# Attention with bias: another order for the first casts, transposes and loads

## The chip, the cores and the metric

The kernel runs on one core of one Trainium2 chip. The metric is the device time of the whole program in microseconds (us), which is some 2 us more than the span of its instructions in the profile. All runs told here are of the state called fast; the one kernel that was run a single time has the state unknown.

## The reference

Four batches of eight heads, 1024 queries and keys, head width 64, with one bias matrix for all heads:

```python
scores = scale * np.matmul(q, k.transpose(0, 1, 3, 2))
scores = scores + bias
attn = np.exp(scores - scores_max) / (np.sum(np.exp(scores - scores_max), ...) + 1e-8)
return np.matmul(attn, v)
```

## The kernel before

The heads are taken in pairs, and for each head, half of the queries and chunk of 128 keys there is one *bank* of scores, 128 keys by 512 queries: 512 banks in all. ScalarE takes the exp of three banks at a time, VectorE multiplies it by the exp of the bias (so the bias is never added), TensorE multiplies by v.

```python
def s_exp(g):
    n = len(slots[g])
    nc.scalar.activation(e_at(slots[g][0], n), open_ps.pop(("S", g))[:, :n, :], ACTF.Exp, scale=scale)
```

Score group S0 has one bank, S1 two, S2, S3 and so on three each. Two score tiles of three banks alternate, so group n+2 can be filled when the exp of group n has ended. Before S0 the first pair must be cast to bfloat16, transposed on TensorE and copied from PSUM, where TensorE's results lie. Four small loads on the queues of SyncE and ScalarE bring it in float32; the second halves of k and q come by GpSimd, straight to bfloat16:

```python
nc.sync.dma_start(out=k0f[:, :, :2]...)      # k chunks 0-1
nc.scalar.dma_start(out=q0f[0]...)           # first half of the queries, head 0: "first q half"
nc.sync.dma_start(out=q0f[1]...)             # the same, head 1: "second q half"
nc.sync.dma_start(out=k0f[:, :, 2:]...)      # k chunks 2-3
# ... (cut)
nc.gpsimd.dma_start(out=kr0[:, :, QC:, :]...)    # k chunks 4-7
nc.gpsimd.dma_start(out=qr0[:, :, QC:, :]...)
nc.gpsimd.dma_start(out=btraw[:, :QC, :], in_=bf_[:, :QC, :])   # half of the bias, 1 MB
# ... (cut)
for i in range(6):                            # warm-up of TensorE
    nc.tensor.matmul(wm[:, i % 3, :], zeros[:, :P], zeros[:], start=True, stop=True)
# ... (cut)
k_first(0, nc.scalar.copy, nc.scalar.copy, "xb")    # cast, transpose, copy of chunks 0-1
c_a = q_first(0, "xa")                              # cast on VectorE, transpose
c_b = q_first(1, "xb")
c_a(); c_b()                                        # copies of q on VectorE
s_fill(0); s_exp(0)
k_first(2, nc.vector.tensor_copy, nc.vector.tensor_copy, "xa")
s_fill(1); s_exp(1)
nc.vector.memset(vall[:, :, :, D:D1], 1.0)
# four memsets of mask, on VectorE
```

Everything after that is put in order by a small plan in the program, which simulates the three engines with fixed costs and emits instructions in that order (constants `COLD`, `T0` and others).

The softmax here doesn't subtract the row's maximum and nothing guards it: scores larger than these inputs give would overflow.

## Time and profile before

| | before |
|---|---|
| time, median of 6 runs | 251.59 us (251.08 to 251.86) |
| span in the profile | 249.4 us |
| busy: ScalarE, TensorE, VectorE | 239.0, 229.8, 220.4 us |
| exp of S0, S1, S2, S3 starts at | 5.77, 7.06, 7.98, 10.60 |
| last exp ends at | 244.40 |

The start times are those of the ACTIVATE records, counted from the start of the span. From S3 on ScalarE runs without a wait, so the table's fourth row decides. TensorE's clock is part of the trace too: its record of full clock begins at 4.65 us in this profile. Before that the matmuls show half: in the warm-up they have a pitch (start to start) of 0.43 us. The column PEclk of the views doesn't show it, as it says 1.00 where there is no record.

### The profile page before, as it was taken

How to read it: one execution, taken by the hardware profiler on the slowest of the kernel's cores; microseconds unless marked ns; L12 is line 12 of the kernel's file. 1: busy time of each engine (PE TensorE's matmuls, PEld its weight loads, DVE VectorE, ACT ScalarE, POOL GpSimd, SP SyncE). 2: the span in 40 equal slices, each digit the busy share in tenths (PEclk: the TensorE clock that was granted, in tenths of full speed). 3: DMA queues.
4: the chain of work that ended last, by engine and by line, in shares of the span. 5: the costliest groups of instructions: out<-in, count | busy, mean ns of one | idle time of the engine just before them, and what ended most of it. 6: DMA issues, size and time to landing. Idle time of an engine off the chain costs nothing.

```text
span 249.4 us, 7171 instructions
## 1 busy us (share of the span) xinstructions
PE 229.8 (92%) x3152; PEld 141.3 (57%) x3152; DVE 220.4 (88%) x380; ACT 239.0 (96%) x180; POOL 52.6 (21%) x72
## 2 busy tenths in 40 slices
PE   6668999999999999999999999999999999999893
PEld 2245656556666556666556556566565555665552
DVE  4519799999999999999999999999999999988884
ACT  4799999999999999999999999999999999999991
POOL 6653304260130221302213055016000000000000
PEclk9999999999999999999999999999999999999998
DMA  7999989699194493921925769629901102020112
GB/s 147 194 205 186 192 90 141 55 158 160 45 147 67 86 105 95 99 88 24 178 49 95 85 83 184 75 87 114 110 33 43 45 0 88 3 84 3 62 46 64
DMA packets 48175, 23.79 MB, mean 95 GB/s; under 512 B 34448, under 2 KB 44048, under 8 KB 47888
## 3 DMA queue, kind: packets, MB, share of 16 engines
q0 software_dynamic: 42272, 14.42, 52.9%
q1 hardware_dynamic: 5584, 8.72, 9.8%
q8 instruction: 24, 0.39, 0.6%
q10 hardware_dynamic: 288, 0.20, 0.3%
q14 instruction: 7, 0.06, 0.1%
HBM read 29.36 MB, written 8.39 MB: 151 GB/s over the span
## 4 chain that ended last, share of the span: by engine, by line
ACT 77%; PE 13%; DVE 5%; issue 2%; DMA 1%; DVEq 0%; ACTq 0%
ACT E L136 74%; PE ps L129 10%; ACT eb L149 3%; PE po L186 2%; DVE E L161 2%; PE px L89 1%; DMA k0f<-in_k_dram 1%; DVE mask L271 1%; DVE E L155 1%; DVE qT L98 1%; DVE kT L102 0%; DVE oall L206 0%; PE px L247 0%; DVE rs L196 0%; DVE qT L255 0%
## 5 line engine op out<-in xcount | busy, mean ns | idle before, releaser
L136 ACT ACTIVATE E<-ps 128x1536 bf16<-128x1536 f32 (+2 forms) x172 | 230.1, 1707 | 2.7 <-PE ps L129 2.7
L129 PE MATMUL ps<-qT,kT 128*128 128x512 bf16 x512 | 138.2, 377 | 10.4 <-ACT E L136 4.7
L186 PEld LDWEIGHTS <-E 128*128 128x128 bf16 x2048 | 83.2, 98 | 38.3 <-DVE E L158 1.6
L158 DVE TENSOR_TENSOR E<-E,eb 128x2048 bf16<-128x2048 bf16 x81 | 97.6, 1216 | 1.1 <-ACT E L136 0.7
L186 PE MATMUL po<-vall,E 128*128 128x65 bf16 x2048 | 92.8, 194 | 1.4 <-DVE E L158 0.5
L129 PEld LDWEIGHTS <-kT 128*128 128x128 bf16 x512 | 45.2, 96 | 43.8 <-issue 7.2
L161 DVE TENSOR_TENSOR E<-E,eb 128x1024 bf16<-128x1024 bf16 x86 | 57.1, 683 | 6.7 <-ACT eb L149 5.6
L75 POOL DMA_DIRECT2D kr<-in_k_dram x15 | 10.5, 701 | 94.6 <-PE px L89 93.4
L81 POOL DMA_DIRECT2D vall<-in_v_dram x32 | 28.1, 883 | 7.4 <-DMA btraw<-in_bias_dram 3.7
L206 DVE TENSOR_TENSOR oall<-po,rs 128x256 f32<-128x256 f32 x63 | 26.7, 424 | 2.2
L98 DVE TENSOR_TENSOR qT<-px,mask 128x1024 bf16<-128x1024 bf16 x31 | 21.3, 686 | 3.7 <-PE px L89 3.1
L102 DVE COPY kT<-px 128x512 bf16<-128x512 bf16 x31 | 13.0, 421 | 2.5 <-PE px L89 2.1
L196 DVE RECIPROCAL rs<-po 128x4 f32<-128x4 f32 x64 | 11.3, 177 | 4.1 <-PE po L186 3.6
L76 POOL DMA_DIRECT2D qr<-in_q_dram x15 | 10.8, 717 | 18.8 <-PE px L89 16.8
L89 PE MATMUL px<-ident,kr 128*64 128x128 bf16 x248 | 12.8, 225 | 0.3 <-DVE oall L206 0.3
L89 PE MATMUL px<-ident,qr 128*64 128x128 bf16 x248 | 12.8, 225 | 0.0
L89 PEld LDWEIGHTS <-qr 128*64 128x64 bf16 x248 | 7.9, 109 | 7.9 <-issue 6.8
L89 PEld LDWEIGHTS <-kr 128*64 128x64 bf16 x248 | 7.9, 109 | 7.1 <-issue 5.5
L149 ACT ACTIVATE eb<-pb 128x2048 bf16<-128x2048 bf16 x4 | 7.5, 1877 | 0.0
L144 PE MATMUL pb<-ident,btraw 128*128 128x128 bf16 x64 | 4.6, 225 | 1.8 <-ACT E L136 0.9
L144 PEld LDWEIGHTS <-btraw 128*128 128x128 bf16 x64 | 4.6, 147 | 2.3 <-issue 2.0
L155 DVE TENSOR_TENSOR E<-E,eb 128x1024 bf16<-128x1024 bf16 (+1 forms) x6 | 4.6, 774 | 0.6 <-ACT E L136 0.6
(36 smaller groups left out, 20.3 us busy)
## 6 DMA issues: line engine op xcount, KB each, us to landing
out_dram<-oall SPq DMA_DIRECT2D x30, 256.0 KB, 2.0
vall<-in_v_dram POOLq DMA_DIRECT2D x32, 128.0 KB, 6.3
kr<-in_k_dram POOLq DMA_DIRECT2D x15, 256.0 KB, 4.0
qr<-in_q_dram POOLq DMA_DIRECT2D x15, 256.0 KB, 5.5
btraw<-in_bias_dram POOLq DMA_DIRECT2D x2, 1024.0 KB, 9.8
out_dram<-oall SPq DMA_DIRECT2D x3, 128.0 KB, 1.7
k0f<-in_k_dram SPq DMA_DIRECT2D x2, 128.0 KB, 3.4
q0f<-in_q_dram ACTq DMA_DIRECT2D x1, 128.0 KB, 2.6
```

The source lines that it names most:

```text
L81: nc.gpsimd.dma_start(out=vall[:, 2 * pr + t, :, :D], in_=vf[pr, :, t])
L89: nc.tensor.transpose(px[t * D:(t + 1) * D, c, :], src[:, t, half * QC + c, :], ident[:])
L98: nc.vector.tensor_tensor(dst[:, :, half * HQ:(half + 1) * HQ], px.rearrange("p c q -> p (c q)").unsqueeze(1).to_broadcast([P, 2, HQ]), ma ...
L102: nc.vector.tensor_copy(dst[:, half * QC:(half + 1) * QC, :], px[:])
L129: nc.tensor.matmul(ps[:, j, :], kT[:, kc, :], qT[:, h, qh * HQ:(qh + 1) * HQ], start=True, stop=b not in late_bias)
L136: nc.scalar.activation(e_at(slots[g][0], n), open_ps.pop(("S", g))[:, :n, :], ACTF.Exp, scale=scale)
L149: nc.scalar.activation(eb[:, qh, k0:k0 + 4, :], open_ps.pop(("B", qh, k0))[:, :4, :], ACTF.Exp)
L158: nc.vector.tensor_tensor(e, e, eb[:, qh, kc:kc + 2, :].unsqueeze(2).to_broadcast([P, 2, 2, HQ]), op=ALU.mult)
L161: nc.vector.tensor_tensor(e, e, eb[:, qh, kc:kc + 1, :].to_broadcast([P, n, HQ]), op=ALU.mult)
L186: nc.tensor.matmul(acc[:, i, :], e[:, 0, i * P:(i + 1) * P], vall[:, 2 * pr + h, kc, :], start=(kc == 0 and i == 0), stop=(kc == NCH - 1), ...
L196: nc.vector.reciprocal(rs[:], acc[:, :, D:D1])
L206: nc.vector.tensor_tensor(oall[:, c0:c0 + QC, :], acc[:, :, :D], rs[:].to_broadcast([P, QC, D]), op=ALU.mult)
```

## The change

The intent is an earlier S0 and an unbroken stream behind it: only k chunk 0 is needed for S0, so it is handled alone; the second q half is cast on ScalarE and transposed into a score tile, so that it no longer waits for a PSUM tile; the memsets of the mask go behind the copy that S3 waits for; k chunks 2-3 move to ScalarE's queue. One warm-up matmul goes, and the plan gets new constants.

```diff
-        nc.sync.dma_start(out=k0f[:, :, 2:]..., in_=kf[0][:, :, 2 * D:QC * D])
+        nc.scalar.dma_start(out=k0f[:, :, 2:]..., in_=kf[0][:, :, 2 * D:QC * D])
@@
-        for i in range(6):
+        for i in range(5):
@@ (helpers cut)
-        k_first(0, nc.scalar.copy, nc.scalar.copy, "xb")
-        c_a = q_first(0, "xa")
-        c_b = q_first(1, "xb")
-        c_a()
-        c_b()
+        nc.scalar.copy(kr0[:, :, 0, :], k0f[:, :, 0, :])
+        nc.vector.tensor_copy(qr0[:, 0, :QC, :], q0f[0][:])
+        nc.vector.tensor_copy(kr0[:, :, 1, :], k0f[:, :, 1, :])
+        nc.scalar.copy(qr0[:, 1, :QC, :], q0f[1][:])
+        pq0 = q_trans(0, ps_x.tile(..., tag="xa", name="px"))
+        pk0 = k_trans(0, 1, "xb")
+        q_out(0, pq0)
+        nc.scalar.copy(kT0[:, :1, :], pk0[:])
+        pq1 = q_trans(1, ps_s.tile(..., tag="s", name="pq")...)
+        nc.vector.tensor_copy(kr0[:, :, 2:QC, :], k0f[:, :, 2:, :])
         s_fill(0)
+        q_out(1, pq1)
         s_exp(0)
-        k_first(2, nc.vector.tensor_copy, nc.vector.tensor_copy, "xa")
+        pk1 = k_trans(1, 1, "xb")
+        nc.vector.tensor_copy(kT0[:, 1:2, :], pk1[:])
+        pk2 = k_trans(2, 2, "xa")
         s_fill(1)
+        nc.vector.tensor_copy(kT0[:, 2:QC, :], pk2[:])
         s_exp(1)
@@
-        for t in range(2):
-            for u in range(2):
-                nc.vector.memset(mask[t * D:(t + 1) * D, u, :], 1.0 if t == u else 0.0)
@@
-        COLD = 9500
+        COLD = 6000
-        T0 = 6200.0
-        t_act, t_pe, t_dve = T0 + 700, T0, T0 + 500
+        T0 = 6000.0
+        t_act, t_pe, t_dve = T0 + 1400, T0 + 600, T0 + 1300
@@ (in the plan, behind the copy of the second half of k)
+                    if (pr, which, half) == (0, 1, 1):
+                        for x in range(2):
+                            for y in range(2):
+                                nc.vector.memset(mask[x * D:(x + 1) * D, y, :], 1.0 if x == y else 0.0)
```

More of the change, by code (lines that the diff above doesn't have):

```diff
@@ L218 @@
         nc.sync.dma_start(out=q0f[1].rearrange("p c d -> p (c d)"), in_=qf[0][:, 1, :QC * D])
-        nc.sync.dma_start(out=k0f[:, :, 2:].rearrange("p t c d -> p t (c d)"), in_=kf[0][:, :, 2 * D:QC * D])
+        nc.scalar.dma_start(out=k0f[:, :, 2:].rearrange("p t c d -> p t (c d)"), in_=kf[0][:, :, 2 * D:QC * D])
         nc.vector.memset(warm[:], 0.0)
@@ L237, with k_trans @@
         wm = ps_s.tile([P, 3, HQ], F32, tag="s", name="wm")
-        for i in range(6):
+        for i in range(5):
             nc.tensor.matmul(wm[:, i % 3, :], zeros[:, :P], zeros[:], start=True, stop=True)
-        def k_first(c0, eng_cast, eng_copy, tag):
-            cs = slice(c0, c0 + 2)
-            eng_cast(kr0[:, :, cs, :], k0f[:, :, cs, :])
-            px = ps_x.tile([P, 2, P], BF, tag=tag, name="px")
-            for c in range(2):
+        def k_trans(c0, n, tag):
+            px = ps_x.tile([P, n, P], BF, tag=tag, name="px")
+            for c in range(n):
@@ L246, in k_first, with q_trans @@
                 for t in range(2):
                     nc.tensor.transpose(px[t * D:(t + 1) * D, c, :], kr0[:, t, c0 + c, :], ident[:])
-            eng_copy(kT0[:, cs, :], px[:])
-        def q_first(t, tag):
-            nc.vector.tensor_copy(qr0[:, t, :QC, :], q0f[t][:])
-            px = ps_x.tile([P, QC, P], BF, tag=tag, name="px")
+            return px
+        def q_trans(t, px):
             for c in range(QC):
                 nc.tensor.transpose(px[t * D:(t + 1) * D, c, :], qr0[:, t, c, :], ident[:])
-            return lambda: nc.vector.tensor_copy(qT0[t * D:(t + 1) * D, t, :HQ],
-                                                 px[t * D:(t + 1) * D, :, :].rearrange("p c q -> p (c q)"))
@@ L258, with q_out @@
-        k_first(0, nc.scalar.copy, nc.scalar.copy, "xb")
-        c_a = q_first(0, "xa")
-        c_b = q_first(1, "xb")
-        c_a()
-        c_b()
+            return px
+        def q_out(t, px):
+            nc.vector.tensor_copy(qT0[t * D:(t + 1) * D, t, :HQ],
+                                  px[t * D:(t + 1) * D, :, :].rearrange("p c q -> p (c q)"))
+        nc.scalar.copy(kr0[:, :, 0, :], k0f[:, :, 0, :])
+        nc.vector.tensor_copy(qr0[:, 0, :QC, :], q0f[0][:])
+        nc.vector.tensor_copy(kr0[:, :, 1, :], k0f[:, :, 1, :])
@@ L263 @@
+        nc.scalar.copy(qr0[:, 1, :QC, :], q0f[1][:])
+        pq0 = q_trans(0, ps_x.tile([P, QC, P], BF, tag="xa", name="px"))
+        pk0 = k_trans(0, 1, "xb")
+        q_out(0, pq0)
+        nc.scalar.copy(kT0[:, :1, :], pk0[:])
+        pq1 = q_trans(1, ps_s.tile([P, 3, 2 * HQ], BF, tag="s", name="pq").rearrange(
+            "p b (c q) -> p (b c) q", q=P)[:, :QC, :])
+        nc.vector.tensor_copy(kr0[:, :, 2:QC, :], k0f[:, :, 2:, :])
         s_fill(0)
+        q_out(1, pq1)
         s_exp(0)
-        k_first(2, nc.vector.tensor_copy, nc.vector.tensor_copy, "xa")
+        pk1 = k_trans(1, 1, "xb")
@@ L285 @@
         NO = len(order)
-        T0 = 6200.0
-        t_act, t_pe, t_dve = T0 + 700, T0, T0 + 500
+        T0 = 6000.0
+        t_act, t_pe, t_dve = T0 + 1400, T0 + 600, T0 + 1300
         filled = []
         act_end = []
-        x_free = {"xa": T0 + 500, "xb": T0}
+        x_free = {"xa": T0 + 400, "xb": T0}
         x_unit = {}
@@ L301 @@
         eb_at = {}
-        exp_at = {0: T0, 1: T0 + 700, 2: T0 + 700}
+        exp_at = {0: T0, 1: T0 + 1400, 2: T0 + 1400}
         mul_at = {}
```

## The prediction

> **What bounds the kernel now.** I read the page from the top: the busy table, the 40 slices, the chain of waits. Then the waits of ScalarE, then the timeline of the first 16 us.
>
> ```profile
> PE 229.8 (92%) x3152; PEld 141.3 (57%) x3152; DVE 220.4 (88%) x380; ACT 239.0 (96%) x180; POOL 52.6 (21%) x72
> ACT  4799999999999999999999999999999999999991
> ACT 77%; PE 13%; DVE 5%; issue 2%; DMA 1%; DVEq 0%; ACTq 0%
> ```
>
> ScalarE (ACT) is the fullest engine, and its row of slices says where it is not full: the first two slices (one is 249.4/40 = 6.2 us) and the last. The view of who waited for whom, for ScalarE alone, has all its waits:
>
> ```profile
> ACT E L136 <- PE ps L129: 2.7, 3, 1.2
> ACT L222 <- PEq L534: 1.2, 1, 1.2
> ACT kr L243 <- DMA k0f<-in_k_dram: 0.9, 1, 0.9
> ACT kT L248 <- PE px L247: 0.5, 1, 0.5
> ```
>
> All of them lie in the start. The exp waited three times for scores, 2.7 us in all. The timeline shows where (start, length, engine, line, what; in brackets the idle time before it and what ended that):
>
> ```profile
> 4.53 0.37 ACT L248 COPY kT<-px 128x256 bf16<-128x256 bf16 x1 [0.52 <-PE px L247]
> 4.89 0.92 DVE L255 COPY qT<-px 64x512 bf16<-64x512 bf16 x2 [0.50 <-PE px L254]
> 5.77 0.60 ACT L136 ACTIVATE E<-ps 128x512 bf16<-128x512 f32 x1 [0.86 <-PE ps L129]
> 5.84 0.29 DVE L243 CAST kr<-k0f 128x256 bf16<-128x256 f32 x1
> 7.06 2.37 ACT L136 ACTIVATE E<-ps 128x1024 bf16<-128x1024 f32 x2 [0.70 <-PE ps L129]
> 8.00 1.67 DVE L271 MEMSET mask<- 64x512 bf16 x4
> 9.69 0.42 DVE L102 COPY kT<-px 128x512 bf16<-128x512 bf16 x1
> 10.60 4.13 ACT L136 ACTIVATE E<-ps 128x1536 bf16<-128x1536 f32 x3 [1.17 <-PE ps L129]
> ```
>
> Call the score groups S0 (one bank), S1 (two), S2, S3 and so on (three each). S0 starts at 5.77, S1 at 7.06, S2 follows it at once and ends at 9.43. S3 waits to 10.60, because its third score matmul needs the second half of the transposed k, and that copy (L102) stood behind four mask memsets on VectorE. The chain says the same:
>
> ```profile
> 8.00 0.48 DVE mask L271
> 9.18 0.48 DVE mask L271
> 9.69 0.44 DVE kT L102
> 10.18 0.40 PE ps L129
> 10.60 5.48 ACT E L136 x4
> ```
>
> After that ScalarE never waits. The busy time in stretches gives 40.00 of 40.00 us from 11 to 51 and full stretches up to 228. From 10.60 to its last end at 244.4 are 233.8 us. The work in it is 168 groups of three banks (169 in the form list, less S2) at a pitch of 1.342 us (5.48 for the four after 10.60 is 4 x 1.342 and an overlap), 225.5; the last group of two banks, 1.1; four bias exps of 1.77, 7.1; sum 233.7. So next to nothing is lost in 234 us. **Everything after S3's start is a fixed stream. What the change is worth is how much earlier S3 starts, less any hole that the stream gets later.** All the idle before 10.60 is some 5 us, 2% of 251.6, so faster by over 2% is nearly out of reach from the outset.
>
> **What the Trainium skill says.** (1) "ScalarE: Activation LUTs", What ACT_TABLE_LOAD costs: an ACTIVATE with immediate scale takes 186 ns + 0.833 ns an element, back-to-back ones overlap by about 93 ns, a table load takes about 1283 ns. At 1536 elements that is 1466 ns, 1373 with overlap. The trace has 1.45 and the 1.342 pitch, and 1.28 for the table load: it agrees within 3%. So the stream has no fat that this change could touch. (2) "TensorE: Matmul & The Clock Gate", What's actually happening: the array runs at half clock until about 3.4 us of activity. The trace agrees: warm-up matmuls from 1.23 at a pitch of 0.43, and from about 4.6 on the pitch of score matmuls is 0.216. One of six warm-up matmuls less ends them at 3.54, not 3.97; the first transposes then follow at about 3.73, a hole of 0.2 us, so I expect the full clock at about the same time. (3) "DMA: Bandwidth & Descriptors", Queues, rings and completion order: each DMA engine takes turns among the queues that have work, packet by packet. In the trace the k transfer that SyncE issued third (1.75) took 3.9 us to land, at 5.65, where the other three took 2.6 to 2.8: it shared the engines with the loads of GpSimd from 1.44 on. On ScalarE's queue it is issued at about 1.2, ahead of them. I expect it at 4.2 to 4.5.
>
> **The change part by part** (times in us from the span's start; what has no duration of its own in the trace is scaled, and marked est.).
> - First cast of ScalarE: 128 elements and not 256. 256 took 0.40 and the one-element warm exp 0.20, so 0.30 (est.): 3.61 to 3.91. Then the q1 cast on ScalarE, 0.40 from its landing. That was 3.91; beside the moved k transfer I take 4.05: done 4.45.
> - TensorE: q0 transposes first, 3.73 to 4.16 (four at half clock took 0.43 at L247); k chunk 0 done by 4.40; q1 transposes 4.50 to 4.90. They write a score tile, so they no longer wait for the k copy to free its bank (before: copy ended at 4.91, transposes began at 4.96).
> - Copies: q0 on VectorE 4.20 to 4.63 (0.43 in the chain), k chunk 0 on ScalarE 4.48 to 4.75 (est. 0.27). S0's matmul 4.95 to 5.33 (0.38), so the exp of S0 starts at **5.37, 0.4 earlier**.
> - VectorE: cast of k chunks 2-3 at 4.65 to 4.94 if landed, q1 copy 4.98 to 5.40, k chunk 1 copy 5.48 to 5.73, chunks 2-3 copy 5.75 to 6.04 (each 0.29 or less in the trace). S1's second matmul starts at 5.87, ends 6.25: exp of S1 at **6.28, 0.8 earlier**. S1 takes 0.92 to the start of S2 (7.06 to 7.98): S2 7.20, S2's end and S3's earliest start 8.55.
> - The four memsets (1.67) now stand behind the copy L102. The copy waits only for its transposes. TensorE has S2's fill to about 6.95, the eight k transposes (issued 1.44, 4.4 to landing, so 5.8) to 7.33, and, new in the instruction order, the eight q transposes (2.27 + 4.2, so 6.5) before S3's fill, to 7.75. L102 runs at 7.37 to 7.80. S3's three matmuls run 7.8 to 8.6: **S3 at 8.65, 1.95 earlier than 10.60**.
> - The memsets then end near 9.5 and the masked q copy follows at 10.2. S6 is the first group to need it, at 8.65 + 3 x 1.34 = 12.7. So they cost the path nothing.
> - Later order: the changed planning constants re-sort the first half of TensorE's and VectorE's lists; the last third stands exactly as before. Three VectorE multiplies of 2048 became six of 1024. A 2048 takes 1.216, two 1024 take 2 x 0.683 with overlap: at most 0.15 each, 0.45 us of an engine with 29 us of idle. Nothing on the path.
> - The tail after the last exp (244.4 to 249.4) is the same list. Sum: 251.61 - 1.95 = **249.7**.
>
> **The rivals.**
> (a) *The stream meets the bias.* Moving 1.95 earlier brings the bias exps forward, but the load does not move, since the DMA queue is full from 5 to 30 us. First half: issued 2.98, 8.7 to landing, 11.7; its transposes can begin when S5 ends, about 12.7. Second half: issued 10.03, 10.8 to landing, 20.9; needed when S9 ends, 8.65 + 8 x 1.34 + 2 x 1.77 - 1.34 = 21.6. For it: that margin is only 0.7, and the 16 transposes take 1.15 of a 1.34 slot, with an AV and a transpose piece ahead in the new order. Against: both landings are before the need. If it bites: 0.2 to 1.0 lost, 249.9 to 250.7.
> (b) *The start is held by another wait.* In its list VectorE has the cast of chunks 2-3 before the q1 copy. If that transfer lands at 5.6 as before, S1 starts near 7.0 and only the memsets' part of the gain is left: S3 at 9.3 to 9.4, 250.4. Against: issued over half a microsecond earlier, on a queue that is otherwise empty by then. Likewise q transposes ahead of S3's fill may cost 0.2 to 0.4 of the 1.95.
> (c) *New holes in the stream from the new order.* TensorE (92%) and VectorE (88%) have little slack early, while multiplies catch up after the first bias exp. For: every piece was re-sorted. Against: the list before was planned with a start that was over 1 us too early for what the trace shows, and it ran without a hole; the new constants (S1's end planned at 7.4, I have 7.2) fit better. It would cost 0.3 to 1.
>
> **Range and chances.** The central case has its errors in S3's start (0.3 either way) and in (a) and (c), which only lose. So 249.7, with 249.2 below (S3 at 8.2) and 250.5 above (b, or a plus c). Over 2% faster would need 246.6, which is all the idle of the start: 0.005. Over 2% slower needs 5 us of new holes: 0.01. Within 2%: 0.985.
>
> **What would show it.** In the changed profile: S0 starting near 5.4, S1 near 6.3, S3 near 8.65 with a wait under 0.2 before it; the q1 transposes beginning before the k copy ends; the k 2-3 cast not waiting for its DMA past 4.6; memsets after L102 and no exp waiting for the masked q copy; ScalarE busy without a hole from S3 to its end, its busy sum unchanged within 0.5; bias exps about 2 us earlier with no wait over 0.2. I am wrong if S3 starts after 9.2, or if a hole of over 0.5 stands at the third bias exp or in the middle.

## The result, and the profile after

The changed kernel takes 251.28 us in the median of six runs (251.0 to 252.24) against 251.59. The ratio is 0.9994, with a 95% interval of 0.9974 to 1.0013: the same. Ratios here are the mean time of one kernel's fast runs over that of the other's in the same rounds, so not quite the ratio of the medians. The prediction was 249.7 with a range of 249.2 to 250.5. The class was right, the number and the range were wrong.

First the page of the changed kernel, the lines for busy time, ScalarE's slices and the chain by engine:

```profile
PE 228.1 (91%) x3096; PEld 141.6 (57%) x3151; DVE 220.5 (88%) x384; ACT 239.1 (96%) x181; POOL 52.6 (21%) x72
ACT  3799999999999999999999999999999999999991
ACT 82%; PE 10%; DVE 3%; issue 2%; DMA 2%; SPq 0%; DVEq 0%; ACTq 0%
```

The stream is untouched: the same busy time of ScalarE to 0.1 us, no slice below 9 between the second and the last. Its waits (in all, times, longest):

```profile
ACT E L136 <- PE ps L129: 1.9, 2, 1.1
ACT L222 <- PEq L544: 1.7, 1, 1.7
ACT qr L260 <- DMA q0f<-in_q_dram: 1.2, 1, 1.2
ACT kr L257 <- DMA k0f<-in_k_dram: 0.3, 1, 0.3
```

There is a new one, 1.2 us for the second q half (`q0f`). And here is the start in the timeline (start, length, engine, line, what, and the idle time before it with what ended it):

```profile
5.05 0.40 ACT L260 CAST qr<-q0f 128x256 bf16<-128x256 f32 x1 [1.22 <-DMA q0f<-in_q_dram]
5.24 0.29 DVE L267 CAST kr<-k0f 128x256 bf16<-128x256 f32 x1 [0.41 <-DMA k0f<-in_k_dram]
5.51 0.64 PE L250 MATMUL pq<-ident,qr 128*64 128x128 bf16 x4 [1.02 <-ACT qr L260]
6.72 0.60 ACT L136 ACTIVATE E<-ps 128x512 bf16<-128x512 f32 x1 [1.10 <-PE ps L129]
7.08 2.10 PE L129 MATMUL ps<-qT,kT 128*128 128x512 bf16 x5
8.15 7.89 ACT L136 ACTIVATE E<-ps 128x1024 bf16<-128x1024 f32 x6 [0.83 <-PE ps L129]
9.57 0.42 DVE L102 COPY kT<-px 128x512 bf16<-128x512 bf16 x1 [0.94 <-PE px L89]
10.04 1.66 DVE L399 MEMSET mask<- 64x512 bf16 x4
```

S0 starts at 6.72 and not at 5.77, nearly 1 us later than before the change. But from S1 on (8.15) there is no wait left: S1, S2 and S3 run one after the other, S3 from 10.57. The memsets are out of the way, as intended. So the kernel lost at the start what it gained behind it, and S3 starts at 10.57 where it started at 10.60. The chain of waits names the two things that it lost by:

```profile
1.24 3.79 DMA q0f<-in_q_dram
5.51 0.64 PE pq L250 x4
7.15 2.05 PE ps L129 x5
9.22 6.82 ACT E L136 x5
```

The one is the load of the second q half, 3.79 us from issue to landing. The views of the tile `q0f`, before and after, give the same (the last figure of each is that load, issued at 1.24 in both kernels):

```profile
DMA to landing us min/median/max: 2.6/2.6/2.7
```

```profile
DMA to landing us min/median/max: 2.5/3.2/3.8
```

The other is TensorE itself. Five score matmuls took 2.10 us in the changed kernel; the same five in the kernel before:

```profile
6.42 1.25 PE L129 MATMUL ps<-qT,kT 128*128 128x512 bf16 x5
```

The view of the tile `ps` in the window from 4 to 10 us has their durations (minimum, median, maximum in ns), before and then after:

```profile
L129 PE MATMUL ps<-qT,kT x8: 376/379/390, 5.4 to 8.4; 128*128 128x512 bf16 x8
```

```profile
L129 PE MATMUL ps<-qT,kT x8: 379/608/634, 6.1 to 9.9; 128*128 128x512 bf16 x8
```

A score matmul takes 0.38 us at full clock and 0.61 to 0.63 at half. In the trace, the clock was full from 4.65 before the change and from 8.84 after it. TensorE had sat idle from 3.54 to 3.75 and from 4.49 to 5.51, while it waited for the casts.

### The profile page after: what moved, and what is told of

Read it like the earlier page. It is cut to its first block, busy times and chain, and to the rows that moved or that the text cites. A ratio compares the mean times of both kernels' runs of the same rounds, so it can differ in the third digit from the quotient of the medians.

```text
span 249.4 us, 7121 instructions
## 1 busy us (share of the span) xinstructions
PE 228.1 (91%) x3096; PEld 141.6 (57%) x3151; DVE 220.5 (88%) x384; ACT 239.1 (96%) x181; POOL 52.6 (21%) x72
## 4 chain that ended last, share of the span: by engine, by line
ACT 82%; PE 10%; DVE 3%; issue 2%; DMA 2%; SPq 0%; DVEq 0%; ACTq 0%
ACT E L136 79%; PE ps L129 7%; ACT eb L149 3%; PE po L186 2%; DMA q0f<-in_q_dram 2%; PE px L89 1%; DVE E L161 1%; DVE E L155 1%; DVE oall L206 0%; DVE qT L98 0%; PE pq L250 0%; DVE rs L196 0%; PE px L245 0%; SPq L216 0%; ACT qr L260 0%
## 5 line engine op out<-in xcount | busy, mean ns | idle before, releaser
L129 PE MATMUL ps<-qT,kT 128*128 128x512 bf16 x457 | 135.3, 381 | 11.3 <-ACT E L136 4.8
L158 DVE TENSOR_TENSOR E<-E,eb 128x2048 bf16<-128x2048 bf16 x78 | 94.1, 1217 | 7.6 <-ACT eb L149 6.4
L161 DVE TENSOR_TENSOR E<-E,eb 128x1024 bf16<-128x1024 bf16 x92 | 61.0, 682 | 0.9 <-ACT E L136 0.7
L102 DVE COPY kT<-px 128x512 bf16<-128x512 bf16 x31 | 13.1, 421 | 3.2 <-PE px L89 3.1
```

What stands on the lines that cost most here:

```text
L102: nc.vector.tensor_copy(dst[:, half * QC:(half + 1) * QC, :], px[:])
L129: nc.tensor.matmul(ps[:, j, :], kT[:, kc, :], qT[:, h, qh * HQ:(qh + 1) * HQ], start=True, stop=b not in late_bias)
L158: nc.vector.tensor_tensor(e, e, eb[:, qh, kc:kc + 2, :].unsqueeze(2).to_broadcast([P, 2, 2, HQ]), op=ALU.mult)
L161: nc.vector.tensor_tensor(e, e, eb[:, qh, kc:kc + 1, :].to_broadcast([P, n, HQ]), op=ALU.mult)
```

## The experiments

Theory A: the moved load took bandwidth from the second q half; the hole that this left on TensorE kept the clock at half. Theory B: the clock was lost by the missing sixth warm-up matmul, whatever the loads do. Each table row further down is from the profile of that run.

### Undo the moved load alone

```diff
-        nc.scalar.dma_start(out=k0f[:, :, 2:]...)
+        nc.sync.dma_start(out=k0f[:, :, 2:]...)
```

> The changed kernel with one line undone: the transfer of k chunks 2-3 goes back to SyncE's queue. Theory A (the moved transfer took the bandwidth of the second q half, which landed at 5.03 and not 3.91, and TensorE's clock came late because of the hole that this left): the second q half lands near 3.9 again, its cast starts by 4.0, score matmuls are at a pitch of about 0.22 us from about 5 us on, the exp of S0 starts near 5.4; the cast of chunks 2-3 then waits for its landing near 5.6 and the exp of S3 starts at 9.2 to 9.6 (changed kernel 10.56). Time about 1.0 to 1.3 us under the changed kernel, 250.0 to 250.4. Theory B (the clock was lost because one warm-up matmul was taken away, whatever the transfers do): q lands at 3.9, but score matmuls stay at a pitch of 0.43 to beyond 8 us, S3 near 10, time within 0.6 us of the changed kernel.

Measured: 251.30 us (250.06 to 252.84), ratio 0.9991 (0.9965 to 1.0016), no gain. The second q half landed at 4.05, as theory A said. The clock stayed at half to 9.52 all the same, as theory B said, and the cast of chunks 2-3, which stands ahead of the second q copy on VectorE, waited for its load:

```profile
5.88 0.29 DVE L267 CAST kr<-k0f 128x256 bf16<-128x256 f32 x1 [0.76 <-DMA k0f<-in_k_dram]
6.68 2.29 PE L129 MATMUL ps<-qT,kT 128*128 128x512 bf16 x5
```

S3 started at 10.61. So the late q half is real and goes with the moved load, but it isn't the whole loss.

### Move the load alone, in the kernel before

```diff
-        nc.sync.dma_start(out=k0f[:, :, 2:]...)
+        nc.scalar.dma_start(out=k0f[:, :, 2:]...)
```

> The kernel before with that one line moved to ScalarE's queue, and nothing else. Theory A: the second q half lands near 5.0, its cast on VectorE starts near 5.05 and not 3.93, everything behind it on VectorE (copies of q, memsets, the copy of the second half of k) comes 0.5 to 1.1 us later, the exp of S3 starts at 11.1 to 11.7 (10.60 before); time 252.1 to 252.7. Theory C (the landing at 5.03 has another cause, such as the other order of reads in the changed kernel): q lands at 3.9, time 251.6 as before.

Measured: 251.51 us (251.41 to 251.96), ratio 0.9999 (0.9987 to 1.0011). The second q half landed at 4.62, 0.7 later than in the kernel before, but S3 moved by only 0.24, to 10.84, as the clock was full from 5.19. The direction was right; the size that I expected (0.5 to 1.1) was not.

### Fill the hole on TensorE

Three warm-up matmuls more, between the transposes of k chunk 0 and those of the second q half.

```diff
+        for i in range(3):
+            nc.tensor.matmul(wm[:, i, :], zeros[:, :P], zeros[:], start=True, stop=True)
         q_out(0, pq0)
```

> The changed kernel with three warm-up matmuls more, put on TensorE between the transposes of k chunk 0 and those of the second q half, where it sat idle from 4.48 to 5.51. The transfers stay as changed. Theory A's second half (the hole kept the clock at half until 8.8): the second q half still lands near 5.0, but from about 4.7 on matmuls of 512 columns are at a pitch of 0.22, the exp of S0 starts near 6.3 (6.72), S1 near 7.1 (8.15), S3 near 9.4 (10.56); time about 1.1 us under the changed kernel, 250.0 to 250.4. If the late clock has another cause: the pitch stays 0.43 until beyond 8 and the time within 0.3 of the changed kernel.

Measured: 251.11 us (250.24 to 251.48), ratio 0.9972 (0.9956 to 0.9988). In the profiled run (250.38) the second q half landed at 5.02, as late as in the changed kernel, but the clock was full from 5.41:

```profile
4.58 1.21 PE L264 MATMUL wm<-zeros 128*128 128x512 bf16 x3
6.68 1.32 PE L129 MATMUL ps<-qT,kT 128*128 128x512 bf16 x5
```

The five matmuls took 1.32 and not 2.10, and S3 started at 9.63 and not at 10.57. With the same loads, the clock is worth 0.94 us between these two profiles, and that is a low estimate: the filling itself held the second q transposes to 5.72, where they had started at 5.51. But two of the six runs lie near 250.3 and the other four at 251.08 to 251.48, which the profile of one run can't explain. (By the spans in the record they are three and three: 248.4 to 248.7 and 249.2 to 249.4.)

### Move the memsets alone, in the kernel before

The four memsets go behind the copy of the second half of k; nothing else of the change is taken.

> The kernel before with the four mask memsets alone moved behind the copy of the second half of k; transfers, casts and planning constants as before. If the prediction's reading of that wait is right: the copy runs near 8.1 to 8.5 and not 9.69, the exp of S3 starts when S2 ends, near 9.45 (10.60); time 250.3 to 250.6. If the memsets only took the place of another wait (the transposes, the landing): S3 stays near 10.6 and the time at 251.6.

Measured: 250.22 us (249.83 to 251.49), ratio 0.9957 (0.9936 to 0.9978), faster by 0.4%.

```profile
7.09 5.05 ACT L136 ACTIVATE E<-ps 128x1024 bf16<-128x1024 f32 x4 [0.69 <-PE ps L129]
8.08 0.42 DVE L102 COPY kT<-px 128x512 bf16<-128x512 bf16 x1
8.56 1.66 DVE L390 MEMSET mask<- 64x512 bf16 x4
```

The copy L102 runs at 8.08 and not at 9.69, and S1, S2 and S3 run without a wait, S3 from 9.34. The prediction's reading of that wait is confirmed, to the size: 1.26 us gained, the 1.17 that S3 had waited and some 0.1 by which exps in a row overlap, with a start that differs by hundredths. This one part is as good as anything that I could make of the whole change.

### The sixth warm-up matmul, with and without the moved load

The first experiment with one line more, six warm-up matmuls in place of five:

> The first experiment (k chunks 2-3 back on SyncE's queue) with the sixth warm-up matmul put back too; it differs from that experiment by this one matmul. There the clock stayed at half to 9.5 although the second q half landed at 4.05, with a hole of 0.49 us on TensorE after the fifth warm-up matmul. Theory B (one warm-up matmul less opens that first hole, and the hole loses the clock): the hole shrinks to 0.1 or less, full clock by 4.7 to 5.2, score matmuls at a pitch of 0.22, S1 near 7.0, S3 at 9.3 to 9.5; time about 1.1 us under the changed kernel. Theory D (the clock is lost by what follows, the 64-column transposes or the later holes): still half clock beyond 8, S3 near 10.5, no gain.

Measured: 250.66 us (250.05 to 252.72), ratio 0.9979 (0.9949 to 1.001). The clock was full from 4.76. S3 came at 9.89, not at 9.3 to 9.5: S0 and S2 gained against the first experiment (5.54 and 8.56 for 5.79 and 9.01), but chunks 2-3 landed at 6.13, and behind their cast the second q copy was late.

```profile
6.15 0.29 DVE L267 CAST kr<-k0f 128x256 bf16<-128x256 f32 x1 [1.08 <-DMA k0f<-in_k_dram]
6.48 0.43 DVE L254 COPY qT<-pq 64x512 bf16<-64x512 bf16 x1
```

That is rival (b) of the prediction. The changed kernel itself is spared it only because its second q half is as late as its chunks 2-3.

The changed kernel with six warm-up matmuls and nothing else:

> The changed kernel with the sixth warm-up matmul back, nothing else; k chunks 2-3 stay on ScalarE's queue. The second q half should land near 5.0 as in the changed kernel, so the hole on TensorE from about 4.5 to 5.5 stays. Theory B (the first hole alone loses the clock): full clock near 4.7, S0 near 6.3, S3 at 9.3 to 9.5, time about 1.1 us under the changed kernel. Theory A (the second hole, left by the late q half, loses it too): clock at half beyond 8, S3 near 10.5, time as the changed kernel.

Measured: 251.37 us (250.09 to 251.97), ratio 0.9981 (0.9957 to 1.0005). In the profiled run (251.58) the first loads were some 0.6 us late by themselves, which opened a hole of 0.48 us behind the sixth matmul; the clock was full from 10.11 only, S3 at 10.85. Two of its runs were at 250.09 and 250.19. This is inconclusive for theory B, and a second hint of two kinds of execution.

The kernel before with five warm-up matmuls:

> The kernel before with five warm-up matmuls in place of six, nothing else; the hole before its first transposes grows from 0.10 to about 0.53. Theory B: the clock stays at half to about 8.8, score matmuls at a pitch of 0.43, S0 near 6.1, S2 later by about 1; S3 is held by the memsets and so moves by 0.3 to 0.8 only: 252.0 to 252.6. Theory D: clock full by 5, S3 at 10.6, time as before.

Measured: 251.88 us (251.69 to 251.95), ratio 1.0009 (0.9997 to 1.0021). The clock was full from 10.67, S3 at 11.14:

```profile
6.97 2.31 PE L129 MATMUL ps<-qT,kT 128*128 128x512 bf16 x5
```

In this profile the late clock, with first loads 0.2 to 0.3 us later than in the kernel before, costs 0.54 us of S3, as the memsets hide much of it.

### The change with its causes mended

Six warm-up matmuls, chunks 2-3 on SyncE's queue, and their cast behind the second q copy:

```diff
         pk1 = k_trans(1, 1, "xb")
         nc.vector.tensor_copy(kT0[:, 1:2, :], pk1[:])
-        pk2 = k_trans(2, 2, "xa")
+        nc.vector.tensor_copy(kr0[:, :, 2:QC, :], k0f[:, :, 2:, :])   # was ahead of s_fill(0)
         s_fill(1)
+        pk2 = k_trans(2, 2, "xa")
```

> What the experiments point to: the changed kernel with the sixth warm-up matmul, k chunks 2-3 on SyncE's queue, and on VectorE the cast of chunks 2-3 behind the q1 copy and the chunk 1 copy (their transposes behind S1's fill on TensorE). If both causes are right: full clock near 4.7, S0 near 5.4, S1 near 6.5, S2 near 7.4, S3 near 8.8; time 249.5 to 250.0, the size of gain that was predicted, 0.3 to 0.6 us under the kernel with the memsets moved alone. If a third wait takes their place: S3 above 9.3 and no better than that kernel.

Measured: 250.37 us (249.97 to 250.75), ratio 0.9954 (0.9941 to 0.9967). S0 at 5.53, S1 at 6.42, S2 at 7.75, S3 at 9.09, clock full from 5.24. S0 and S1 are where I expected them, S2 and S3 0.3 later, since chunks 2-3 landed at 6.04:

```profile
6.06 0.29 DVE L272 CAST kr<-k0f 128x256 bf16<-128x256 f32 x1
7.75 4.13 ACT L136 ACTIVATE E<-ps 128x1536 bf16<-128x1536 f32 x3 [0.30 <-PE ps L129]
```

The time is no better than with the memsets alone.

### The same kernels again

Up to here, the clock had been late in each profile that had a hole of 0.48 us or more on TensorE before 5.6, and early in the others. The next runs tested that rule. The changed kernel, word for word:

> The changed kernel word for word, for a second profile and more times on the chip of the runs beside it. If the late clock and the late second q half belong to the kernel and are no accident of one execution: the second q half lands at 4.6 to 5.1, a hole of about 0.5 us or more stands on TensorE before 5.6, full clock only after 8.5, S3 at 10.3 to 10.9, median 251.0 to 251.6. If they were an accident: full clock by 5.5, S3 near 9.5, median near 250.3.

Measured: 251.41 us, ratio 0.9981 (0.9961 to 1.0001). Five runs lie at 251.05 to 251.83, but the profiled one took 250.05, inside the predicted range. Its timeline:

```profile
5.08 0.41 PE L250 MATMUL pq<-ident,qr 128*64 128x128 bf16 x4 [0.46 <-ACT qr L260]
6.04 1.32 PE L129 MATMUL ps<-qT,kT 128*128 128x512 bf16 x5
6.74 5.05 ACT L136 ACTIVATE E<-ps 128x1024 bf16<-128x1024 f32 x4 [0.29 <-PE ps L129]
```

The clock was full from 4.48, though TensorE had idled 0.35 and 0.46 us before 5.1; the second q half landed at 4.60; S3 started at 8.99, 1.58 us earlier than in the other profile of the same program. So the late clock is not fixed by the program; it differs between executions.

This profile also shows what an early S3 meets next, the third bias exp, from the timeline of ScalarE and from the chain of waits in the window from 14 to 32:

```profile
23.82 1.88 ACT L149 ACTIVATE eb<-pb 128x2048 bf16<-128x2048 bf16 x1 [0.42 <-PE pb L144]
```

```profile
9.67 12.87 DMA btraw<-in_bias_dram
```

The second half of the bias landed at 22.54, and ScalarE waited for its transposes. Of the 1.58 us gained at S3, about 0.5 are lost, most of it here: from S3 to the end of the last exp are 234.32 us and not 233.80.

The mended kernel with five warm-up matmuls:

> The mended kernel (six warm-up matmuls, chunks 2-3 on SyncE's queue, their cast later on VectorE) with five warm-up matmuls in place of six, so that the one matmul is tested where the transfers are not in the way. The first hole on TensorE becomes 0.35 to 0.5 us. In ten profiles so far the full clock came by 5.4 where no hole before 5.6 was over 0.36, and at 8.8 to 10.7 where one was 0.48 or more. If that is the rule here: with a hole over 0.45 full clock after 8.5, S3 at 9.9 to 10.5 (9.09 with six), median 0.5 to 1.2 us over the mended one, 250.9 to 251.6; with a hole under 0.36, as the mended one. If the sixth matmul does not matter here: 250.4.

Measured: 250.59 us (249.94 to 251.29), ratio 0.9956 (0.9937 to 0.9976). The profiled run, at 251.29 its slowest, had a hole of only 0.33 us and yet full clock only from 10.27, S3 at 10.73. Other runs of the same program took 249.94 and 250.03. My rule of one hole of a certain length fell with it: late here with 0.33, early in the profile above with 0.35 and 0.46.

The kernel before again, one look:

> The kernel before word for word, one look, for a second profile of its start. Expected as the first: second q half landed near 3.9, no hole over 0.25 us on TensorE before 5.6, full clock by 5.3, S3 at 10.5 to 10.9.

Measured: 251.11 us, clock full from 3.90, the second q half landed at 3.87, S3 at 10.55. Like the first profile but for the clock, which came even before the earliest time that I had expected and moved S3 by 0.05 only.

### Chunks 2-3 by GpSimd

The mended kernel with the load and the cast of chunks 2-3 replaced by a first, converting load of GpSimd:

```diff
-        nc.sync.dma_start(out=k0f[:, :, 2:]..., in_=kf[0][:, :, 2 * D:QC * D])
+        nc.gpsimd.dma_start(out=kr0[:, :, 2:QC, :]..., in_=kf[0][:, :, 2 * D:QC * D])
         nc.gpsimd.dma_start(out=kr0[:, :, QC:, :]...)
@@
-        nc.vector.tensor_copy(kr0[:, :, 2:QC, :], k0f[:, :, 2:, :])
```

> The mended kernel with k chunks 2-3 loaded by GpSimd's first transfer, straight to bfloat16, so that neither a third transfer on the fast queues nor a cast on VectorE is needed. In the mended kernel S2 waited for them (landed 6.04, S2 at 7.75 though S1 ended its pitch at 7.35). If the sharing of the engines is what made them late: they land near 5.0 to 5.4, S2 follows S1 at 7.3 to 7.4, S3 at 8.65 to 8.8, as was predicted for the change itself; time 249.6 to 250.1. If the second halves of k and q, now one issue later, take over: S3 above 9.2, time as the mended kernel or worse.

Measured: 250.76 us (250.52 to 251.78), ratio 0.9962 (0.9948 to 0.9976). Chunks 2-3 landed at 4.99 and the second q half at 3.83, the loads were as hoped. But the second half of q, now one issue later, landed at 9.22, and its transposes stand ahead of S3's fill:

```profile
9.26 0.41 PE L89 MATMUL px<-ident,qr 128*64 128x128 bf16 x8 [0.73 <-DMA qr<-in_q_dram]
```

The clock was full from 7.17, S3 came at 10.46, and the second half of the bias landed at 24.31, for 0.73 us of waiting at the third bias exp. A transfer saved in one place was paid for in two others.

### Making the clock early or late on purpose

Three runs for the open point, whether the runs of the changed kernel that have no profile were slow for the clock. Nine warm-up matmuls, six first and three behind the transposes of k chunk 0:

> The changed kernel with six warm-up matmuls and three more behind the transposes of k chunk 0, so that TensorE has dense work from 1.2 to 5.5; transfers as changed. If the late clock is what the gain was lost to: full clock by 5.5 (7.3 at worst), S3 at 9.0 to 9.7, and nearly all timed runs at 249.9 to 250.6, where one run in twelve of the changed kernel lies; median 250.3. If the time comes from elsewhere (the late second q half alone): S3 above 10, median 251.2.

Measured: 250.64 us (250.25 to 251.28), ratio 0.9974 (0.9959 to 0.9989). The clock came at 6.63 with no hole at all before it. At half clock the three extra matmuls themselves held the second q transposes to 5.96, and S3 came at 10.13. Better than the changed kernel, worse than expected: the filling has a price where the clock is late anyway.

The mended kernel with one such matmul more:

> The mended kernel (six warm-up matmuls, chunks 2-3 on SyncE's queue and their cast later on VectorE) with one warm-up matmul more behind the transposes of k chunk 0. Clock: full by 5.3 in nearly every execution, S3 at 9.0 to 9.4, median 250.0 to 250.4, no run over 250.8. If the clock is not what spreads the runs: median 250.4 with single runs at 251 as in the other kernels.

Measured: 250.42 us (250.1 to 251.46), ratio 0.997 (0.9952 to 0.9987). Clock full from 5.96, S3 at 9.70; two of six runs above 251. Both miss my expectation. But the two above 251 are slow outside the program: the spans of all six lie at 247.9 to 248.7 (see below the table).

The changed kernel without warm-up:

> The changed kernel without its five warm-up matmuls of 512 columns (three of one column stand in for the tile). TensorE is idle until about 3.7, so the clock is late in every execution: full at 7.1 to 10.7, score matmuls at a pitch of 0.43 until then. If the clock is the cause: S3 at 10.3 to 11.0 and all times at 251.0 to 252.0, with none near 250.1, as the bulk of the changed kernel's runs. If warm-up has no part in it: times as the changed kernel with an occasional fast run, or much slower than it.

Measured: 251.66 us (250.96 to 252.03), ratio 1.0009 (0.9995 to 1.0023). The clock was full from 10.48, S3 at 11.16. None of the six runs is below 250.96. Of the twelve runs of the changed kernel that I have, eleven are at 251.0 and above.

### All profiles in one table

"q1" and "k2-3" are the landings of the second q half and of k chunks 2-3, "clock" is the time from which it was full; the last column is the profiled run's own time, in us as the rest.

| kernel | q1 | k2-3 | clock | S0 | S1 | S3 | time |
|---|---|---|---|---|---|---|---|
| before | 3.91 | 5.64 | 4.65 | 5.77 | 7.06 | 10.60 | 251.22 |
| before, again | 3.87 | 5.76 | 3.90 | 5.53 | 7.01 | 10.55 | 251.11 |
| before, load moved | 4.62 | 4.99 | 5.19 | 5.98 | 7.30 | 10.84 | 251.51 |
| before, five warm-ups | 3.97 | 5.82 | 10.67 | 6.34 | 8.04 | 11.14 | 251.72 |
| before, memsets moved | 3.92 | 5.79 | 4.70 | 5.81 | 7.09 | 9.34 | 250.11 |
| changed | 5.03 | 5.22 | 8.84 | 6.72 | 8.15 | 10.57 | 251.41 |
| changed, again | 4.60 | 4.91 | 4.48 | 5.85 | 6.74 | 8.99 | 250.05 |
| changed, hole filled | 5.02 | 5.22 | 5.41 | 6.49 | 7.38 | 9.63 | 250.38 |
| changed, six warm-ups | 4.63 | 4.97 | 10.11 | 6.33 | 7.75 | 10.85 | 251.58 |
| changed, load undone | 4.05 | 5.85 | 9.52 | 5.80 | 7.73 | 10.61 | 251.15 |
| both undone | 4.03 | 6.13 | 4.76 | 5.54 | 7.64 | 9.89 | 250.65 |
| mended | 3.88 | 6.04 | 5.24 | 5.53 | 6.42 | 9.09 | 249.97 |
| mended, five warm-ups | 3.86 | 5.74 | 10.27 | 5.63 | 6.84 | 10.73 | 251.29 |
| changed, no warm-up | 4.87 | 5.16 | 10.48 | 6.56 | 7.99 | 11.16 | 251.73 |
| changed, dense warm-up | 5.03 | 5.22 | 6.63 | 6.99 | 7.88 | 10.13 | 250.72 |
| mended, dense warm-up | 3.94 | 5.75 | 5.96 | 6.24 | 7.13 | 9.70 | 251.26 |
| mended, chunks 2-3 by GpSimd | 3.83 | 4.99 | 7.17 | 5.66 | 6.88 | 10.46 | 251.78 |

Two columns sort the rest. The second q half lands at 3.86 to 4.05 wherever chunks 2-3 are on SyncE's queue behind it, and at 4.60 to 5.03 wherever they are on ScalarE's. And every kernel with the memsets moved has S3 at 10.57 or later with a clock after 8.8, and at 9.89 or earlier with a clock before 6; the two clocks in between, 6.63 and 7.17, go with 10.13 and 10.46 (the latter held by a load too).

The record also lists the span of every timed run, and the time hides it in part: a run's time is its span and 1.7 to 3.1 us more. Of the changed kernel's twelve runs, eleven have spans of 249.2 to 249.9 and one has 248.3. Without warm-up the six spans are 249.2 to 250.3. The mended kernel with dense warm-up has 247.9 to 248.7; its two times above 251 have 2.8 and 3.0 us outside the span.

## Why the prediction was wrong

**What bounds the kernel: right.** ScalarE's stream from S3 to the end of the last exp is 233.80 us before and after (244.40 - 10.60 and 244.37 - 10.57), and the tail behind it is the same. The time follows S3's start, and a gain of over 2% was out of reach.

**The memsets: right, in mechanism and size.** They run behind the copy L102, no exp waits for the masked q, and alone they brought S3 from 10.60 to 9.34.

**The landing: wrong by 1 us.** The step was "beside the moved k transfer I take 4.05" for the second q half, and 4.2 to 4.5 for chunks 2-3. They landed at 5.03 and 5.22. I had read the long way of chunks 2-3 in the kernel before (3.9 us) as a cost that an earlier issue on another queue avoids. The load beside it pays for that, and S0 needs that one and not chunks 2-3. (Whether by the other queue or by the issue at 1.20 and not 1.75, the runs don't separate.) "Trainium Kernel Development and Optimization", the section Key Constraints of the Trainium skill, has it in a sentence: loads issued from different engines run on the same 16 DMA engines and interleave, and only the issue time is saved. The trace agrees: chunks 2-3 gained 0.4 us (5.64 to 5.22), the second q half lost 1.1 (3.91 to 5.03).

**The clock: wrong, and at least about half of the loss.** The step was "so I expect the full clock at about the same time". It came at 8.84. That step counted one hole of 0.2 us and planned TensorE almost without a gap from 3.73 to 4.90; the first hole was there, but the late landing left a second one, from 4.49 to 5.51. From the landing on, the loss adds up in the profile: the second q cast ended 1.0 late (5.45, planned 4.45), its transposes took 0.64 in place of 0.40 and S0's matmul 0.61 in place of 0.38, which is 1.47 in all, where S0 came 1.35 later than predicted (6.72 in place of 5.37). The k transposes and the matmuls of S1 and S2 at a pitch of 0.43 make it 1.92 at S3: 10.57 in place of 8.65. With the loads as they are and the clock early, S3 was at 9.63; so at least some 0.9 of the 1.9 is the clock, and the rest is mostly the landing.

My error was to take the 3.4 us for a delay from the first matmul and to look at one execution only. The section that the prediction cites, What's actually happening in "TensorE: Matmul & The Clock Gate", says that the window is free-running and that the point at which the clock rises differs from run to run. The traces agree: 8.84 and 4.48 for the same program, 3.90 and 4.65 for the kernel before. The clock records bear the window out: the stretch of full clock is 238.93, 242.35 or 245.76 us long in all 17 profiles, which is 70, 71 or 72 times 3.413. So here the clock changes on a grid of 3.413 us, and the grid lies differently against each start. Counting back from the rise by such steps, with TensorE's busy time from the view by stretches:

| profile | step | busy | full clock after it |
|---|---|---|---|
| before | 1.24 to 4.65 | 3.31 | yes |
| changed | 2.01 to 5.42 | 2.27 | no |
| changed | 5.42 to 8.84 | 3.33 | yes |
| changed, again | 1.07 to 4.48 | 2.90 | yes |
| changed, dense warm-up | -0.20 to 3.21 | 1.99 | no |
| changed, dense warm-up | 3.21 to 6.63 | 3.41 | yes |

In the changed kernel's first profile both holes fell, but for 0.1 us, into one step, and full clock came one step of 3.41 us later. In the second profile the step ended before the second hole (4.62 to 5.08). And the dense warm-up's clock, late without a hole, fits too: a step ended at 3.21, when its matmuls had run for only 2 us. How much work suffices stays open: over all profiles, steps with 2.67 to 3.41 us busy were followed by full clock, and steps with up to 3.06 were not. A single hole isn't the measure.

That the eleven slower runs of the changed kernel had a late clock is argued, not shown: only the profiled runs have a record that dates the rise. For it: the two profiles differ so, and the spans do. The span less S3 is 238.8 us in both kernels' first profiles, so with spans of 249.2 to 249.9 S3 was at about 10.4 to 11.1 in those eleven (an estimate); with the memsets moved, no profile has S3 past 10.13 with a clock before 7. Without warm-up no span is below 249.2. The changed kernel with dense warm-up, which should have made it certain, came out between the two (250.64).

**The rivals.** (a), the stream meets the bias, is real: a wait of 0.42 us in the fast execution of the changed kernel (S3 at 8.99), and of 0.73 with chunks 2-3 by GpSimd (S3 at 10.46). "The load does not move" was wrong. I had the landing at 20.9, as in the kernel before (20.86); it was 22.27 and 22.54 in the changed kernel's two profiles. It goes with the memsets: the first half of the bias landed at 11.66 to 11.91 in the four profiles without that move and at 12.14 or later in the others, the second at 20.86 to 21.18 and at 21.43 or later. No run shows why. An S3 earlier than these would probably wait longer here. (b), chunks 2-3 ahead of the second q copy on VectorE, is what the load's undoing ran into. (c), new holes from the new order, didn't come.

So where the expected 1.95 us went: the memsets gave about 1.3, the new first steps about 0.25 more when all is mended (9.34 to 9.09), and the late q half with the late clock took as much away. In the execution where the clock was early, the predicted time and the measured one are 249.7 and 250.05.

## What to carry to other kernels

Before moving a load to another queue to have it earlier, list what else lands in the same microsecond and which of the two the next step needs first. In a start of a few microseconds TensorE's clock is a quantity of its own: take more than one profile, see the durations of equal matmuls, and expect a kernel with holes there to have more than one time. Look at the span of each timed run beside its time. And try the parts of a change one by one: here one moved block of memsets gave 0.4%, and the rest of the change gave it back.

## What the Trainium skill lacked or had wrong

- "TensorE: Matmul & The Clock Gate", What's actually happening: it puts the spread of the transition at about half a microsecond, though a note in it has one kernel with 6, 11 or 14 slow matmuls. For programs with transposes and waits in their first microseconds the full clock came between 3.90 and 10.67 us, and at 4.48 or 8.84 for one and the same program. It doesn't say how much work in a window suffices: a step with 2.67 us of busy TensorE was followed by full clock, one with 3.06 was not.
- The same section calls the cost of the ramp under 1% of a usual kernel. Here it was 0.94 us of 251 (0.4%) with equal loads, which agrees, but that is nearly as much as the best versions gained in the timed runs (1.1 to 1.2 us by their ratios).
- "DMA: Bandwidth & Descriptors", Queues, rings and completion order: it names the taking of turns but has no figure for its effect at a start. A third load of 128 KB on the second queue put off the landing of its neighbour from 3.86 to 4.05 us to 4.60 to 5.03.
- No page that I read has it: a strided memset of 256 elements on VectorE was preceded by 0.87 to 0.89 us of idle time, with no wait that the profile shows, in each kernel whose timeline I read there.
